# First modulation vectors of a hybrid DeltaNet / gMLP step: weights as the stationary operand

## The chip, the cores and the metric

The kernel runs on one core of a Trainium2 chip. A core has TensorE (matrix products, with a weight load and a matmul instruction for each product), VectorE (DVE), ScalarE (ACT), GpSimd (POOL) and SyncE (SP), which here issues the DMA transfers. The metric is the device time of one execution in microseconds. A profile is one execution taken by the hardware profiler; the time before is the median of three runs.

## The reference

One layer of a backbone over 128 context tokens and 2048 latent tokens, with a model width of 1024. Both kinds of token go through a norm that is scaled and shifted by modulation vectors, a mixer, a gated addition, a second modulated norm and an MLP. What the change touches is the modulation:

```python
def modulation(cond, w_mod_l, b_mod_l):
    m = jax.nn.silu(cond) @ w_mod_l + b_mod_l
    return jnp.split(m[:, None, :], N_MOD, axis=-1)
...
    sh1, sc1, ga1, sh2, sc2, ga2 = mod
    h = rmsnorm(x, norm_mix_l) * (1.0 + sc1) + sh1
```

There are two conditioning vectors, `c_ctx` for the context and `c` for the latent tokens. `w_mod` is 1024 × 6144 in float32. Its first 1024 columns give the shift `sh1`, the next 1024 the scale `sc1`. The kernel needs both as columns: feature number on the partitions, because the normed tokens stand feature-major when they are scaled.

## The kernel before

The kernel is written in Tile. Instructions are written in program order, and a scheduler orders them on each engine before the program is built, by a simulated timeline; each engine then runs its own list in order, and so does SP with its transfers. Tiles come from pools: a tile with `tag` and `bufs` takes one of so many buffers, and a new tile of that tag waits until the oldest is free.

The whole is staged. The first stage (lines 267 to 802, to about 445 us) computes the conditioning vectors, the modulation, the normed and modulated tokens and the projections to q, k, v. Later stages do the gMLP, the DeltaNet scans, the output projection and the MLP. The change lies in the first 40 us.

The steps there, in the order of the code:

- `scond` (line 296) holds silu of the two conditioning vectors, 128 partitions × 8 k-steps × 2 vectors.
- `mod_load` (line 313) issues eight transfers of 128×512 float32 raw weights (256 KB each). It is called for `m0` (shift, first 512 features), `m1` (scale, first 512), and then `m2` and `m3` (shift and scale, second 512), each with its own eight buffers of the pool `wp`.
- `mod_columns` (line 317) turns one such set into columns. Line 321 does eight products: the stationary operand is `scond[:, k, :]` (128×2), the moving operand the raw weights (128×512), and the result, 2×512, gathers in a PSUM bank `pm`. ACT copies it to SBUF as `mrow` (line 323). Four transposes (line 326) write its four 2×128 pieces as 128×2 into a second PSUM bank of the same tag, `pc` in the code and `pm` in the profile. DVE adds the bias from `vec` (line 329) and, for a scale, forms (1 + sc1) · norm weight (line 333), into `b1` or `a1`.
- `xh` (line 363) are ten boundary tokens, loaded by five small transfers and normed; eight transposes (line 373) and a copy make `hal`. `xh` takes one of the three buffers of the tag `x` in the pool `p1`. The same three buffers then serve the three token tiles of the first block (line 377); the third of these waits for the transposes of `xh`.
- `norm_rows` (line 298) norms a token tile: ACT squares and sums, DVE and POOL form the inverse root, DVE scales.
- `first_half(0)` needs the columns of `m0` and `m1`; `column(k)` (line 455) transposes the normed tokens (line 468), scales and shifts them on ACT (line 470) and splits them on DVE into a high and a low part (lines 473, 474). `project(k)` multiplies them with split weights by `mm3` (lines 217 to 219). The first three projections run k = 0 to 3, then come `m2` and `m3`, then k = 4 to 7 in the code's order (lines 728 to 738).
- `pm1()` (line 169) gives one of two PSUM banks of the tag `pm`.

A product in plain float32 is built as two weight loads and two matmul instructions; one in float32r as one of each.

Of the kernel before, what the change touches and what calls it, by code (L numbers as in the profile page):

```python
# [8 lines left out]
F32 = mybir.dt.float32  # L9
# [8 lines left out]
P = 128  # L18
D = 1024
KT = D // P  # L20
# [41 lines left out]
def hybrid_step(  # L62
# [7 lines left out]
    V, A, G, T = nc.vector, nc.scalar, nc.gpsimd, nc.tensor  # L70
# [41 lines left out]
    ident = cp.tile([P, P], F32, name="ident")  # L112
# [49 lines left out]
    scond = cp.tile([P, KT, 2], F32, name="scond")  # L162
# [6 lines left out]
    def pm1():  # L169
        return pmp.tile([P, 512], F32, tag="pm", name="pm", bufs=2)  # L170
# [96 lines left out]
    with ExitStack() as ph:  # L267
        p1 = ph.enter_context(tc.tile_pool(name="p1", bufs=2, reuse_waits="tile"))
        pf = ph.enter_context(tc.tile_pool(name="p1f", bufs=2, reuse_waits="tile"))
# [46 lines left out]

        def mod_columns(raws, half, dst, bias, scaled):

            pm = pm1()
            for k in range(KT):  # L320
                T.matmul(pm[0:2, :], scond[:, k, :], raws[k], start=k == 0, stop=k == KT - 1)  # L321
            row = p1.tile([2, 512], F32, tag="mrow", name="mrow", bufs=1)
            A.copy(row, pm[0:2, :])
            pc = pm1()
            for i in range(4):
                T.transpose(pc[:, 2 * i : 2 * i + 2], row[:, i * P : (i + 1) * P], ident[0:2, 0:2])
            ks = slice(half * 4, half * 4 + 4)
            d = dst[:, :, ks]
            V.tensor_tensor(out=d, in0=pc[:, 0:8].rearrange("p (k c) -> p c k", c=2),
                            in1=bias[:, ks].unsqueeze(1).to_broadcast([P, 2, 4]), op=ALU.add)  # L330
            if scaled:
                for cd in range(2):
                    V.scalar_tensor_tensor(out=dst[:, cd, ks], in0=dst[:, cd, ks], scalar=1.0,
                                           in1=vec[:, 16 + half * 4 : 20 + half * 4], op0=ALU.add, op1=ALU.mult)
# [23 lines left out]
        convw = vec[:, 32:68].rearrange("p (w a) -> p w a", w=3)  # L358
        m1 = mod_load(0, D)
        mod_columns(m0, 0, b1, vec[:, 0:8], False)  # L360


        xh = p1.tile([P, D], F32, tag="x", name="xh", bufs=3)[0:10, :]
        for m in range(5):
            r0 = 255 + 384 * m
            load(out=xh[2 * m : 2 * m + 2, :], in_=x_sample[0, r0 : r0 + 2, :])
# [9 lines left out]
        for t in BLOCKS[0]:  # L376
            x = p1.tile([P, D], F32, tag="x", name="x", bufs=3)
# [341 lines left out]
        m3 = mod_load(1, D)  # L719
        wr = load_w1(1, range(4))  # L720
        mod_columns(m1, 0, a1, vec[:, 8:16], True)
        W1[1] += [split_w(r) for r in wr]
        first_half(0)
# [5 lines left out]
        for k in range(4):  # L729
            cols[k]()  # L730
            for u in us:
                u["main"][k]()
        mod_columns(m2, 1, b1, vec[:, 0:8], False)
        mod_columns(m3, 1, a1, vec[:, 8:16], True)
        W1[1] += [split_w(r) for r in wk]
# [1016 lines left out]
    raws, sops = {}, {}  # L1752
# [91 lines left out]
    for m, (n, i, u, q) in enumerate(todo):  # L1844
# [20 lines left out]
        if i in (1, 5, 6) and mm < 28:  # L1865
            while pending and mm >= pending[0][0] + 2:
                _, k, r = pending.pop(0)
# [60 lines left out]
```

## Time and profile before

| | |
|---|---|
| runs | 2690.73, 2695.26 (median), 2696.66 us |
| profiled execution | 2696.7 us, of which the span from first to last instruction is 2695.0 us |
| mean granted TensorE clock | 0.993 |
| PE busy | 2628.5 us, 98% of the span, 15698 instructions |
| PEld (weight loads) busy | 2192.3 us, 81%, 15698 instructions |
| DVE busy | 1866.8 us, 69% |
| ACT busy | 1245.5 us, 46% |
| POOL busy | 229.5 us, 9% |
| DMA | 580.91 MB, mean 216 GB/s |

How the profile is read: PE is TensorE's matmuls and PEld its weight loads, which overlap them. The ends of matmuls are modelled, and they are pipelined, so a busy PE is not PE at its peak; the distance from one start to the next tells the pace. In a row of the timeline stand the start, the length, the engine, the line, the operation, out<-in, the shape and the count; behind it in brackets how long the engine had been idle and what it waited for. In the shape of a matmul or weight load, `128*2` is the rows and columns of the stationary operand, and behind it stands what was streamed or loaded. In a row of a table of stretches stand the stretch (us), its length, the busy time of each engine with its instruction count (PE, PEld, DVE, ACT, POOL), the granted clock, the busy share of the DMA engines and the GB/s that they moved. The granted clock has no entry ahead of the first change of the clock and shows 1.00 there.

### The profile page before, as it was taken

The numbers are of one execution on the slowest core, as the hardware profiler recorded it, in microseconds if no ns is written. First come the engines' busy times: TensorE is split into PE (matmuls) and PEld (weight loads), VectorE is DVE, ScalarE is ACT, GpSimd is POOL, SyncE is SP. The second block draws the span as 40 slices with busy tenths as digits, with TensorE's granted clock in tenths as the row PEclk, the third lists the DMA queues.
The fourth block names the chain that finished last, engine by engine and source line by source line (L and its number), as shares of the span: only waits on it lengthen the run. The fifth ranks groups of instructions, "written<-read, shape, count | busy, mean of one in ns | idle before, by whom it ended". The sixth has DMA issues, their size and how long they took to land.

```text
span 2695.0 us, 45202 instructions
## 1 busy us (share of the span) xinstructions
PE 2628.5 (98%) x15698; PEld 2192.3 (81%) x15698; DVE 1866.8 (69%) x3909; ACT 1245.5 (46%) x3092; POOL 229.5 (9%) x448
## 2 busy tenths in 40 slices
PE   8999999999999899999999999999999999999998
PEld 5999997788887787778887788888888787888887
DVE  5867656877777878885688775665565547774874
ACT  4655555555555656763355543332342432342441
POOL 3111203111111111110000000000000000000000
PEclk9999999999999999999999999999999999999999
DMA  8867539555555657885877797433459979876772
GB/s 297 279 202 224 183 113 299 177 157 161 160 162 157 204 191 232 269 279 181 285 221 228 212 313 228 122 104 106 121 170 371 329 265 309 272 243 215 235 252 94
DMA packets 569388, 580.91 MB, mean 216 GB/s; under 512 B 35693, under 2 KB 401693, under 8 KB 565575
## 3 DMA queue, kind: packets, MB, share of 16 engines
q1 hardware_dynamic: 569158, 578.03, 67.2%
q8 instruction: 123, 2.02, 0.3%
q14 instruction: 107, 0.87, 0.1%
HBM read 398.14 MB, written 179.74 MB: 214 GB/s over the span
## 4 chain that ended last, share of the span: by engine, by line
PE 86%; DVE 6%; DMA 5%; issue 1%; ACT 1%; POOL 0%; SPq 0%; DVEq 0%; POOLq 0%; ACTq 0%
PE f L219 17%; PE f L217 17%; PE f L218 17%; PE pj L217 6%; PE pj L219 6%; PE pj L218 6%; PE pd L959 3%; PE pm L217 1%; PE pm L219 1%; PE pm L218 1%; PE pm L321 1%; PE pt L575 1%; PE pd L1136 1%; PE pd L1137 1%; DMA qT<-qT_d 1%
## 5 line engine op out<-in xcount | busy, mean ns | idle before, releaser
L217 PE MATMUL f<-hop,zH 128*128 128x512 f32 x960 | 376.5, 393 | 1.2 <-ACT zH L1444 1.2
L218 PE MATMUL f<-hop,zH 128*128 128x512 f32 x960 | 377.1, 393 | 0.0
L219 PE MATMUL f<-hop,zL 128*128 128x512 f32 x960 | 376.9, 393 | 0.0
L217 PE MATMUL f<-hop,wH 128*128 128x512 f32 x896 | 354.0, 397 | 0.0
L219 PE MATMUL f<-hop,wL 128*128 128x512 f32 x896 | 351.3, 392 | 0.0
L218 PE MATMUL f<-hop,wH 128*128 128x512 f32 x896 | 351.1, 392 | 0.0
L1444 ACT CAST zH<-zraw 128x512 fp32r<-128x512 f32 x240 | 146.6, 620 | 287.2 <-DVE zraw L1438 86.4
L217 PEld LDWEIGHTS f<-hop,zH 128*128 128x128 f32 x960 | 180.3, 188 | 43.7 <-ACT zH L1444 1.6
L219 PEld LDWEIGHTS f<-hop,zL 128*128 128x128 f32 x960 | 180.3, 188 | 41.9 <-issue 0.9
L218 PEld LDWEIGHTS f<-hop,zH 128*128 128x128 f32 x960 | 180.2, 188 | 41.8 <-issue 0.9
L1438 DVE TENSOR_TENSOR zL<-zraw,zH 128x512 fp32r<-128x512 f32 x240 | 162.9, 686 | 69.1 <-ACT zH L1444 57.7
L219 PEld LDWEIGHTS f<-hop,wL 128*128 128x128 f32 x896 | 168.5, 188 | 37.7
L218 PEld LDWEIGHTS f<-hop,wH 128*128 128x128 f32 x896 | 168.8, 188 | 35.2
L217 PEld LDWEIGHTS f<-hop,wH 128*128 128x128 f32 x896 | 168.8, 188 | 34.7
L217 PE MATMUL pj<-kH,wH 128*128 128x386 f32 (+2 forms) x568 | 190.5, 338 | 0.3 <-DVE kH L473 0.3
L219 PE MATMUL pj<-kH,wL 128*128 128x386 f32 (+2 forms) x568 | 190.3, 335 | 0.0
L218 PE MATMUL pj<-kL,wH 128*128 128x386 f32 (+2 forms) x568 | 189.5, 334 | 0.0
L176 POOL TENSOR_TENSOR r<-rsq,nhalf 128x1 f32<-128x1 f32 (+1 forms) x38 | 23.0, 606 | 1499.3 <-DVE rsq L175 1499.3
L1438 DVE TENSOR_TENSOR wL<-raw,wH 128x512 fp32r<-128x512 f32 x112 | 76.0, 687 | 76.0 <-ACT wH L1444 74.9
L523 DVE SCALAR_TENSOR_TENSOR cv<-pj,vec,cv 128x384 f32<-128x384 f32 (+2 forms) x164 | 87.1, 539 | 58.7 <-ACT cv L520 57.4
L217 PEld LDWEIGHTS pj<-kH,wH 128*128 128x128 f32 x568 | 107.2, 189 | 4.6 <-issue 4.2
L217 PE MATMUL pj<-wH,hH 128*128 128x512 f32 x248 | 109.8, 443 | 0.0
(398 smaller groups left out, 6088.3 us busy)
## 6 DMA issues: line engine op xcount, KB each, us to landing
zraw<-z_d SPq DMA_DIRECT2D x212, 256.0 KB
raw<-in_w_ff_dram SPq DMA_DIRECT2D x128, 256.0 KB
hop<-hop_d SPq DMA_DIRECT2D x28, 1024.0 KB
z_d<-c SPq DMA_DIRECT2D x96, 256.0 KB
zraw<-s_d SPq DMA_DIRECT2D x96, 256.0 KB
raw<-in_w_mod_dram SPq DMA_DIRECT2D x80, 256.0 KB
r<-in_w_ff_dram SPq DMA_DIRECT2D x80, 256.0 KB
s_d<-s SPq DMA_DIRECT2D x64, 256.0 KB
```

The source lines that it names most:

```text
L176: G.tensor_tensor(out=out, in0=t[:np_, :n], in1=nhalf[:np_, :n], op=ALU.pow)
L217: T.matmul(ps, lh, rh, start=first and i == 0, stop=False, skip_group_check=more)
L218: T.matmul(ps, lh, rl, start=False, stop=False, skip_group_check=more)
L219: T.matmul(ps, ll, rh, start=False, stop=last and i == n - 1, skip_group_check=more)
L321: T.matmul(pm[0:2, :], scond[:, k, :], raws[k], start=k == 0, stop=k == KT - 1)
L523: V.scalar_tensor_tensor(out=cv[:, o : o + m], in0=ps[:, s + sh : s + sh + m], scalar=convw[:, w, j : j + 1], in1=cv[:, o : o + m], op0=AL ...
L575: T.matmul(ps[:, i * P : (i + 1) * P], kTt[:, i * P : (i + 1) * P], rhs[:, i * P : (i + 1) * P], start=True, stop=True)
L959: T.matmul(p[:, h, :], lhs[:, h, :], rhs[:, h, :], start=True, stop=True)
L1136: T.matmul(p[:, h, :], u["qT"][:, h, :], s[:, h, :], start=True, stop=False)
L1137: T.matmul(p[:, h, :], u["QK"][:, h, :], u["vn"][:, h, :], start=s is None, stop=True)
L1438: V.tensor_tensor(out=out, in0=a, in1=b, op=op)
L1444: A.copy(h, src)
```

## The change

In `mod_columns` the operands change places. Each 128×512 raw weight tile is taken in four pieces of 128×128, each piece is the stationary operand, and the moving operand is `scond[:, k, :]`, 128×2. The result of piece i is 128×2, feature-major, in columns 2i and 2i+1 of one PSUM bank, gathered over the eight k-steps. So the copy to `mrow` and the four transposes go, and with them the second PSUM bank of each call. A call had eight products and four transposes; it now has 32 products. The steps on DVE behind it are as before.

The boundary tokens `xh` no longer take a buffer of the tag `x`; they have a buffer of their own in the pool `pf`.

```diff
         def mod_columns(raws, half, dst, bias, scaled):
 
-            pm = pm1()
+            pc = pm1()
             for k in range(KT):
-                T.matmul(pm[0:2, :], scond[:, k, :], raws[k], start=k == 0, stop=k == KT - 1)
-            row = p1.tile([2, 512], F32, tag="mrow", name="mrow", bufs=1)
-            A.copy(row, pm[0:2, :])
-            pc = pm1()
-            for i in range(4):
-                T.transpose(pc[:, 2 * i : 2 * i + 2], row[:, i * P : (i + 1) * P], ident[0:2, 0:2])
+                for i in range(4):
+                    T.matmul(pc[:, 2 * i : 2 * i + 2], raws[k][:, i * P : (i + 1) * P], scond[:, k, :],
+                             start=k == 0 and i == 0, stop=k == KT - 1 and i == 3)
             ks = slice(half * 4, half * 4 + 4)
             d = dst[:, :, ks]
...
-        xh = p1.tile([P, D], F32, tag="x", name="xh", bufs=3)[0:10, :]
+        xh = pf.tile([P, D], F32, tag="xh", name="xh", bufs=1)[0:10, :]
```

## The prediction

> **What bounds the kernel now.** I read the page first, then the chain of waits, then the timeline and the table of stretches for the first 130 us, because the change touches nothing later.
>
> ```profile
> span 2695.0 us, 45202 instructions
> PE 86%; DVE 6%; DMA 5%; issue 1%; ACT 1%; POOL 0%; SPq 0%; DVEq 0%; POOLq 0%; ACTq 0%
> ```
>
> The chain that ended last is TensorE work for 86% of the span. So what the change does to TensorE's time in its stage should reach the end almost in full, if TensorE is the bound in that stage and behind it. The timeline of PE in the stage (start, us):
>
> ```profile
> 4.56 9.38 PE L321 MATMUL pm<-raw,scond 128*2 128x512 f32 x16 [4.56 <-DMA raw<-in_w_mod_dram]
> 15.01 7.03 PE L321 MATMUL pm<-raw,scond 128*2 128x512 f32 x16
> 21.97 0.66 PE L373 MATMUL pt<-ident,xh 10*128 10x10 f32 x8
> 22.56 0.53 PE L468 MATMUL pt<-ident,x 128*128 128x128 f32 x2
> 23.36 7.03 PE L321 MATMUL pm<-raw,scond 128*2 128x512 f32 x16
> 31.11 0.41 PE L326 MATMUL pm<-ident,mrow 2*128 2x2 f32 x4 [0.72 <-ACT mrow L323]
> 31.44 7.03 PE L321 MATMUL pm<-raw,scond 128*2 128x512 f32 x16
> 39.19 0.41 PE L326 MATMUL pm<-ident,mrow 2*128 2x2 f32 x4 [0.46 <-ACT mrow L323]
> 40.57 0.59 PE L217 MATMUL pj<-kH,wH 128*128 128x388 f32 x2 [0.32 <-DVE kH L473]
> ```
>
> The four calls of mod_columns (I name them by their weights m0, m1, m2, m3) fill PE from 4.56 to 39.60, and only then come the projections. A float32 product is two instructions here, hence x16 for eight k. The last three calls run at 0.43 us per instruction, the first takes 9.38 us instead of 7.03. What follows, in stretches (PE, PEld, DVE, ACT and POOL busy, granted clock, DMA share, GB/s):
>
> ```profile
> 38.50:41.00 2.50, 1.72 (x9) 1.11 (x10) 1.48 (x10) 1.89 (x4) 0.00 (x0) 1.00 1.02 343
> 41.00:50.00 9.00, 9.00 (x59) 8.82 (x59) 8.93 (x31) 6.89 (x16) 4.40 (x12) 1.00 0.81 280
> 50.00:60.00 10.00, 10.00 (x60) 9.97 (x59) 9.96 (x29) 6.22 (x14) 4.61 (x9) 1.00 0.56 179
> 80.00:90.00 10.00, 9.43 (x53) 8.19 (x53) 9.09 (x21) 8.91 (x30) 0.85 (x1) 1.00 0.65 190
> 90.00:100.00 10.00, 9.21 (x60) 8.60 (x59) 8.10 (x18) 5.05 (x15) 0.00 (x0) 1.00 0.99 310
> 100.00:110.00 10.00, 9.96 (x63) 9.48 (x62) 5.04 (x13) 8.97 (x30) 4.31 (x23) 1.00 0.91 302
> 110.00:120.00 10.00, 9.72 (x64) 9.21 (x63) 8.19 (x18) 6.15 (x17) 3.93 (x12) 1.00 1.02 341
> 120.00:130.00 10.00, 9.76 (x57) 9.36 (x56) 9.56 (x16) 2.97 (x6) 0.00 (x0) 1.00 0.96 307
> ```
>
> From 41 on PE has no slack to swallow a shift: idle between 80 and 130 is 0.57 + 0.79 + 0.04 + 0.28 + 0.24 = 1.9 us. Shifts of the first stage are carried on.
>
> **Part one: what is removed.** Sixty-four L321 instructions, and behind each call one ACT copy of 0.57 us and four L326 transposes, which PE waits for:
>
> ```profile
> 30.48 0.57 ACT L323 COPY mrow<-pm 2x512 f32<-2x512 f32 x1 [7.82 <-PE pm L321]
> 31.10 0.32 PEld L326 LDWEIGHTS pm<-ident,mrow 2*128 2x128 f32 x4 [1.65 <-ACT mrow L323]
> ```
>
> From the last product of m2 to the first of m3 PE gives 31.44 − 30.39 = 1.05 us to this hop, the same behind m0; behind m1 other transposes fill it, and behind m3 it is 39.60 − 38.47 = 1.1.
>
> **Part two: what is added.** Each call becomes 8 × 4 products of two columns, 64 instructions instead of 16, each with a weight load of 128×128 float32: 256 loads in all. Two moving columns cost next to nothing (0.43 us for 512), so the load sets the pace. The rows nearest to it:
>
> ```profile
> 427.88 0.53 PEld L654 LDWEIGHTS pt<-scr,mcum 128*128 128x128 f32 x4
> 38.40 0.14 PEld L468 LDWEIGHTS pt<-ident,x 128*128 128x128 f32 x1 [0.86 <-DVE wL L192]
> 427.64 0.19 PEld L219 LDWEIGHTS pj<-kH,wL 128*128 128x128 f32 x1
> 929.05 1.81 PEld L959 LDWEIGHTS pd<-vn,kt 128*128 128x128 f32 x8
> 1111.86 0.33 PEld L219 LDWEIGHTS pm<-wH,oL 128*128 128x128 f32 x1
> ```
>
> L654 has the same form (plain float32 weights, 128×128) before a moving operand of only 68 columns: (0.53 − 0.19) / 3 = 0.113 us from load to load. L326's transposes give a lower bound, with 0.14 for one load as in L468's transpose: (0.32 − 0.14) / 3 = 0.06. But a load for a transpose is shorter than the 0.19 of a product in L219, so I take 0.113. At full clock then 256 × 0.113 = 28.9 us, against 64 × 0.43 = 27.5: no gain on the products themselves, only the hops. The last two rows stand in stretches at half clock (in the table below): one load takes 0.33 instead of 0.19, and eight come (1.81 − 0.33) / 7 = 0.211 us apart. Bounds 0.211 and 2 × 0.113 = 0.226; I take 0.216, as those eight also stream 128 columns each: 256 × 0.216 = 55.3 us (54.0 to 57.9).
>
> **Which clock holds** decides the sign. The first call starts at half clock; its loads are 0.86 us apart and become 0.43 apart behind 9.4 us:
>
> ```profile
> 6.22 0.13 PEld L321 LDWEIGHTS pm<-raw,scond 128*2 128x2 f32 x1 [0.73 <-issue]
> 7.08 0.13 PEld L321 LDWEIGHTS pm<-raw,scond 128*2 128x2 f32 x1 [0.73 <-DMA raw<-in_w_mod_dram]
> 9.92 0.09 PEld L321 LDWEIGHTS pm<-raw,scond 128*2 128x2 f32 x1 [0.34 <-issue]
> 10.35 0.09 PEld L321 LDWEIGHTS pm<-raw,scond 128*2 128x2 f32 x1 [0.34 <-issue]
> ```
>
> Later the clock falls to half and rises again in steps of 3.41 us. The table of such stretches, the granted clock third from the right:
>
> ```profile
> 473.55:476.97 3.42, 3.07 (x17) 1.76 (x17) 3.42 (x12) 1.93 (x7) 0.61 (x1) 0.50 0.71 259
> 476.97:480.38 3.41, 2.37 (x19) 1.55 (x18) 3.41 (x12) 3.41 (x9) 1.75 (x3) 1.00 0.25 82
> 920.70:924.11 3.41, 1.84 (x25) 1.21 (x24) 3.41 (x9) 3.41 (x15) 0.40 (x1) 1.00 0.98 331
> 924.11:927.53 3.42, 1.83 (x20) 1.44 (x20) 3.42 (x14) 1.96 (x7) 0.90 (x3) 1.00 0.51 182
> 927.53:930.94 3.41, 2.96 (x24) 2.76 (x23) 3.41 (x16) 1.66 (x4) 1.70 (x3) 0.50 0.37 111
> 930.94:934.35 3.41, 3.41 (x31) 3.11 (x30) 3.20 (x11) 1.01 (x3) 0.90 (x1) 0.50 0.28 79
> 1111.85:1115.26 3.41, 3.41 (x9) 2.65 (x8) 3.31 (x11) 0.25 (x1) 1.62 (x2) 0.50 1.04 369
> ```
>
> Each stretch sets the clock of the next. 920.70 and 924.11 have the same matmul time (1.84 and 1.83); the second has more weight loading (1.44 against 1.21), yet behind it the clock falls. 927.53 has loads in 2.76 of 3.41 us and the clock stays at half; 473.55 has loads in only 1.76, but a little more matmul time (3.07 against 2.96), and the clock rises. So loads don't seem to count, streaming does. That rests on four stretches, and the profile's matmul time has modelled ends, so it is a lean and no proof. The new products stream 2 columns, 0.43 × 2 / 512 = 0.0017 us, per load: under 2% of the time. If only streaming counts, the clock never rises until the projections come.
>
> The Trainium skill, "TensorE: Matmul & The Clock Gate", section "Part 1: The HAM clock gate (the "warmup" mystery)", has the same gate: default half rate, lifted by a busy window of about 3.4 us. It does not say whether a weight load is busy time; read so that it is, its sum would be that of the first rival, read as streaming only, that of the forecast.
>
> **The sum at half clock.** m0 starts at 4.56 as now (first weights landed; a k-step takes 8 × 0.216 = 1.7 us, more than its weights take to land). 4.56 + 55.3 + 2 × (0.66 + 0.53) for the L373 and L468 transposes = 62.3, against 39.60: **+22.7**. The gap from 39.60 to the first projection at 40.57 goes, as the first half's columns are built while m2 and m3 run: **−1.0**. About nine further L468 transposes move into the slow stretch, at some 0.1 us more each (half of 0.211): **+1.0**. The clock lifts one to two stretches of 3.41 us into the projections, half of that lost: 1.7 to 3.4, **+2.3**. Of the 1.9 us idle later a half is regained by loads that have landed earlier: **−1.0** (0 to −1.9). Together **+24.0 us**: 2695.0 of span and 1.7 around it, 2696.7, become 2720.7. The median of the runs is 1.4 under the profiled one, so I predict **2719**; by the bounds 2712 to 2724.
>
> **The xh tile** gets a buffer of its own, so the third x load need not wait for xh's. In SP's order it stands at 27.81, two weight loads late:
>
> ```profile
> 16.03 10.02 SPq L182 DMA_DIRECT2D raw<-in_w_mod_dram  x16
> 27.81 0.33 SPq L378 DMA_DIRECT2D x<-in_x_sample_dram  x1
> 31.80 1.28 ACT L191 CAST wH<-raw 128x512 fp32r<-128x512 f32 x2 [0.75 <-DMA raw<-in_w_in_dram]
> ```
>
> Ahead of the sixteen weight loads, it delays m2, m3 and w_in by its 512 KB, at the 343 GB/s above 1.5 us; PE is still in m1 then, so I cost it at nothing (at full clock w_in lands before m3 ends at 36.9, below: nothing too). The DVE and ACT steps behind the products stay (L329, L333).
>
> **Rivals.** *Weight loads count as busy, full clock from about 9.4 us* (not slower). m0: 22 loads at half rate until 9.34, 42 × 0.113 more: 14.1. m1 21.3, transposes 22.5, m2 29.7, m3 36.9 instead of 39.60; with the 1.0 gap gone −3.7: 2693.0, by the median 2691.6. For it: PE would be occupied without a pause, and matmul shares as low as 1.84 of 3.41 kept the clock. Against: the two pairs above.
>
> *The load is as short as a transposed one, 0.062, at full clock.* Then arrivals bound the stage: w_in's first split begins at 31.80, and with it the projections at about 33.2 instead of 40.57: −7.4, 2689 (median 2688). For it: L326 has 128 columns too. Against: L654.
>
> *The clock rises in between* because column transposes and projections of the first half are ordered between m1 and m3, which streams enough: half way between the two cases, about 2705. Against it: w_in lands only at 31.8.
>
> **Chances.** Half clock 0.58, in between 0.06, full clock 0.28, short loads 0.08. Differences under 0.2% (5.4 us) I call the same. Full clock at −3.7 is mostly within that, a third of it beyond: same 0.19; faster 0.08 + 0.09 = 0.17; slower 0.58 + 0.06 = 0.64. The range takes in the full-clock case and the upper bound of the forecast: 2690 to 2724; the forecast's own is 2712 to 2724.
>
> **What would show it.** Loads of L321's successor 0.21 apart until past 60 us, the granted clock 0.50 or lifted only there, first L217 at about 62: right. Loads 0.11 apart behind 9.4 us: the first rival. 0.06: the second. A first L217 at 62 with an end less than 20 us late would refute the step that nothing behind takes up a shift.

## The result, and the profile after

The changed kernel takes 2720.9 us (median of five runs, 2718.5 to 2725.7), the kernel before, beside it, 2693.8 us (2690.7 to 2696.7). The ratio is 1.0104, with a 95% interval of 1.0092 to 1.0115: about 1% slower. The profiled execution took 2720.5 us, 2718.8 of it span, 23.8 us more than before.

The head of the profile after:

```profile
span 2718.8 us, 45547 instructions
...
PE 82%; DMA 7%; DVE 7%; issue 2%; ACT 1%; SPq 1%; POOL 0%; DVEq 0%; POOLq 0%; ACTq 0%
```

TensorE still holds most of the chain that ended last. In the head that chain now runs through transfers (start, us):

```profile
25.42 5.31 DMA raw<-in_w_mod_dram
30.75 5.39 DMA raw<-in_w_in_dram
...
38.71 2.77 POOL kH L460
41.53 1.01 PE pj L217 x2
```

So the first projection is not released by the new products but by its own weights and by kH, into which POOL copies a boundary column (line 460), about as early as before (40.57). What the new products lose there shows behind it, where they and the projections share TensorE. The timeline of the weight loads of the exchanged products, now line 322 (start, us):

```profile
4.01 18.00 PEld L322 LDWEIGHTS pm<-scond,raw 128*128 128x128 f32 x84 [4.01 <-DVE abW L311]
22.98 9.46 PEld L322 LDWEIGHTS pm<-scond,raw 128*128 128x128 f32 x44
32.85 6.95 PEld L322 LDWEIGHTS pm<-scond,raw 128*128 128x128 f32 x32
45.67 3.42 PEld L322 LDWEIGHTS pm<-scond,raw 128*128 128x128 f32 x26
...
58.25 8.14 PEld L322 LDWEIGHTS pm<-scond,raw 128*128 128x128 f32 x60
```

The first 84 loads come (18.00 − 0.33) / 83 = 0.213 us apart (one load at half clock takes 0.33 us); so do the next 76. The 26 loads behind 45.67 come about 0.13 apart on average. The first two calls last until 32.4, in the kernel before until 22.0. The stretches between show why the pace changes (columns as before; the clock has no entry ahead of its first change, here at 46.56, and shows 1.00 there):

```profile
43.15:46.56 3.41, 3.41 (x15) 3.31 (x15) 2.15 (x6) 2.13 (x5) 2.51 (x12) 1.00 1.00 323
46.56:49.97 3.41, 3.41 (x30) 3.41 (x31) 3.20 (x9) 2.00 (x5) 1.78 (x3) 1.00 1.05 383
49.97:53.39 3.42, 3.42 (x15) 3.42 (x15) 2.16 (x6) 1.64 (x5) 3.42 (x8) 0.50 0.81 270
53.39:56.80 3.41, 3.41 (x12) 3.41 (x11) 2.78 (x9) 3.19 (x7) 0.64 (x3) 0.50 0.60 197
60.22:63.63 3.41, 3.41 (x33) 3.41 (x32) 0.00 (x0) 0.00 (x0) 0.00 (x0) 1.00 0.00 0
63.63:67.04 3.41, 3.41 (x18) 3.41 (x19) 0.45 (x4) 0.00 (x0) 0.00 (x0) 0.50 0.00 0
```

From 43.15 to 46.56 projections of 388 columns and four transposes run, and the clock is up in the next stretch. That stretch is mostly two-column products, and behind it the clock is down. Projections from 51.85 on lift it a second time, at 56.80, and the last sixty loads let it fall again, at 63.63, although PE and PEld show 3.41 of 3.41 us busy. A busy engine in the profile is thus not a busy engine for the clock.

The projections begin here, still at half clock (388 columns, 0.52 us each instead of 0.34):

```profile
41.53 1.01 PE L217 MATMUL pj<-kH,wH 128*128 128x388 f32 x2 [1.64 <-POOL kH L460]
43.74 0.52 PE L218 MATMUL pj<-kL,wH 128*128 128x388 f32 x1
...
45.03 1.05 PE L465 MATMUL pt<-ident,x 128*128 128x128 f32 x4
45.88 3.29 PE L322 MATMUL pm<-scond,raw 128*128 128x2 f32 x26
```

The stage's last projection, first in the changed kernel, then before:

```profile
456.89 0.28 PE L219 MATMUL pj<-kH,wL 128*128 128x258 f32 x1
```

```profile
433.70 0.28 PE L219 MATMUL pj<-kH,wL 128*128 128x258 f32 x1
```

It is 23.2 us later. The end is 23.8 later. Some 21 us are lost in the first 70 us, about 2 around 145 us, and the loss is carried through the rest.

### The profile page after: what moved, and what is told of

It is laid out like the page before. It is cut to its first block, busy times and chain, and to the rows that moved or that the text cites. A ratio compares the mean times of both kernels' runs of the same rounds, so it can differ in the third digit from the quotient of the medians.

```text
span 2718.8 us, 45547 instructions
## 1 busy us (share of the span) xinstructions
PE 2653.5 (98%) x15874; PEld 2241.9 (82%) x15874; DVE 1865.4 (69%) x3909; ACT 1245.9 (46%) x3088; POOL 229.9 (8%) x448
## 4 chain that ended last, share of the span: by engine, by line
PE 82%; DMA 7%; DVE 7%; issue 2%; ACT 1%; SPq 1%; POOL 0%; DVEq 0%; POOLq 0%; ACTq 0%
PE f L219 16%; PE f L217 16%; PE f L218 16%; PE pj L217 6%; PE pj L219 6%; PE pj L218 6%; PE pd L956 2%; DMA qT<-qT_d 1%; PE pm L217 1%; PE pm L219 1%; PE pm L218 1%; DMA raw<-in_w_mod_dram 1%; PE pt L572 1%; PE pd L1133 1%; PE pd L1134 1%
## 5 line engine op out<-in xcount | busy, mean ns | idle before, releaser
L217 PE MATMUL f<-hop,zH 128*128 128x512 f32 x960 | 376.5, 393 | 1.2 <-ACT zH L1441 1.2
L217 PE MATMUL f<-hop,wH 128*128 128x512 f32 x896 | 354.8, 397 | 0.0
L217 PEld LDWEIGHTS f<-hop,zH 128*128 128x128 f32 x960 | 180.4, 188 | 43.7 <-ACT zH L1441 1.6
L217 PEld LDWEIGHTS f<-hop,wH 128*128 128x128 f32 x896 | 169.1, 189 | 34.9
L217 PE MATMUL pj<-kH,wH 128*128 128x386 f32 (+2 forms) x568 | 192.9, 341 | 3.5 <-POOL kH L460 1.6
L217 PEld LDWEIGHTS pj<-kH,wH 128*128 128x128 f32 x568 | 108.1, 191 | 8.7 <-issue 4.9
L217 PE MATMUL pj<-wH,hH 128*128 128x512 f32 x248 | 110.3, 445 | 0.0
```

The costliest lines, as they stand in the source:

```text
L217: T.matmul(ps, lh, rh, start=first and i == 0, stop=False, skip_group_check=more)
```

## The experiments

The theory: a product of two columns streams so little that TensorE's clock neither rises nor stays up, and the weight loads then take twice as long. The rivals: the loads or the number of products cost the time by themselves; the new place of `xh` or the new order does; or only the rise of the clock fails. Eleven kernels were run. All ratios are to the kernel before, run beside them on the same chip. "Stage end" is the start of the last 258-column projection in the profile, 433.7 us before and 456.9 in the changed kernel; it comes from one execution, while the runs of one kernel spread over up to 13 us.

| run | edit | median us | ratio, 95% interval | stage end |
|---|---|---|---|---|
| e1 | xh alone | 2694.6 | 0.9999 (0.9989 to 1.0008) | 434.1 |
| e2 | exchanged operands alone | 2716.8 | 1.0089 (1.0074 to 1.0104) | 451.4 |
| e5 | 32 columns | 2720.3 | 1.0106 (1.0080 to 1.0132) | 452.2 |
| e4 | 64 columns | 2707.8 | 1.0052 (1.0037 to 1.0067) | 444.4 |
| e6 | 88 columns | 2712.7 | 1.0077 (1.0057 to 1.0098) | 446.1 |
| e3 | 112 columns | 2694.9 | 1.0008 (0.9999 to 1.0017) | 434.0 |
| e7 | two calls old, two new | 2715.4 | 1.0085 (1.0054 to 1.0115) | 446.7 |
| e8 | 112 columns, one set on DVE | 2718.7 | 1.0094 (1.0072 to 1.0117) | 458.3 |
| e9 | before, other bank | 2696.3 | 1.0016 (1.0006 to 1.0025) | 440.2 |
| e10 | 112 columns, early products | 2700.2 | 1.0026 (1.0014 to 1.0037) | 434.4 |
| e11 | before, other bank, early products | 2696.0 | 1.0016 (1.0007 to 1.0024) | 438.4 |

**e1: xh alone.** The kernel before with

```diff
-        xh = p1.tile([P, D], F32, tag="x", name="xh", bufs=3)[0:10, :]
+        xh = pf.tile([P, D], F32, tag="xh", name="xh", bufs=1)[0:10, :]
```

> The kernel before with one edit alone: xh in its own buffer, products as before. Theory (the loss is the half clock that the two-column products cannot lift): no loss, 2690 to 2697 us, clock lifted at about 9 us as before. Rival (the earlier third x load reorders the stage and delays weights on the one DMA queue): 5 us or more slower than before, 2699 or above.

Ratio 0.9999: this edit by itself costs nothing.

**e2: the exchange alone.** The changed kernel with `xh` back in the tag `x`.

> The changed kernel with xh back in the shared buffers: operands exchanged alone. Theory (half clock): 2716 to 2724 us, loads 0.21 us apart wherever the clock shows 0.50 or has not risen yet. Rival (much of the loss comes with the xh tile): 2710 or below.

1.0089 against 1.0104: most of the loss, or all, as the intervals of the two overlap. The exchange is what costs. Whether `xh` adds something once the operands are exchanged stays open.

**e3: 112 columns instead of 2.** The stationary operand, the loads and their number stay. The two columns are repeated 56 times in the moving operand, and 110 of each 112 results are never read:

```diff
-                    T.matmul(pc[:, 2 * i : 2 * i + 2], raws[k][:, i * P : (i + 1) * P], scond[:, k, :],
+                    T.matmul(pc[:, 112 * i : 112 * i + 112].rearrange("p (a c) -> p a c", c=2),
+                             raws[k][:, i * P : (i + 1) * P],
+                             scond[:, k, :].unsqueeze(1).to_broadcast([P, 56, 2]),
                              start=k == 0 and i == 0, stop=k == KT - 1 and i == 3)
...
-            V.tensor_tensor(out=d, in0=pc[:, 0:8].rearrange("p (k c) -> p c k", c=2),
+            V.tensor_tensor(out=d, in0=pc[:, 0:448].rearrange("p (k w) -> p w k", w=112)[:, 0:2, :],
```

> The changed kernel, but the moving operand repeats the two columns 56 times, so that every weight load is followed by 112 streamed columns; 110 of them are never read. Loads and instructions are the same in number. Theory (only streaming lifts the clock): 112 columns at half clock stream for 0.19 of some 0.216 us, 87% of the time, above the 0.75 or so that lifted the clock in the kernel before; the clock rises about 9 to 11 us, loads come 0.11 us apart, and the time falls by 24 to 30 us to 2690 to 2697, although TensorE streams 56 times as many columns. Rival (the loads, or the number of instructions, or the new order cost the time by themselves): 2716 or above.

2694.9 us, against 2720.9 for two columns: streaming 56 times as much takes the whole loss away. Its loads, and the stretches around the rise:

```profile
4.11 16.05 PEld L322 LDWEIGHTS pm<-scond,raw 128*128 128x128 f32 x126 [4.11 <-DVE abW L311]
...
27.33 10.80 PEld L322 LDWEIGHTS pm<-scond,raw 128*128 128x128 f32 x96
```

```profile
4.72:8.13 3.41, 3.41 (x18) 3.41 (x18) 0.00 (x0) 0.00 (x0) 3.41 (x30) 1.00 0.98 304
8.13:11.55 3.42, 3.42 (x32) 3.42 (x32) 0.17 (x1) 0.00 (x0) 0.21 (x2) 1.00 1.05 384
```

18 products in one stretch, 32 in the next: the clock rose at 8.13, behind one stretch. The later 96 loads come (10.80 − 0.19) / 95 = 0.112 us apart. The loads don't cost the time by themselves; the clock at which they run does. The new order is not ruled out by this run alone, because the order changed with the width: here all 256 products run ahead of the first projection (38.08), in the changed kernel 36 instructions of the projections run ahead of the last product. With 64 columns, below, it is also 36, and the stage still ends 12.5 us earlier than with two. The 10.7 us that are left there are no more than the half clock accounts for: 160 loads run at it ahead of the first projection, 160 × 0.10 = 16 us.

**e4, e5, e6: 64, 32 and 88 columns.** The same edit with another width.

> As the run with 112 columns, with 64. Theory (a stretch of 3.41 us must stream about three quarters to lift the clock, and 0.38 to keep it): 64 columns stream 0.107 of 0.216 us, half of the time, too little to lift it and enough to keep it. So the first calls run at half clock until projections lift it, and what follows keeps full clock: between, 2702 to 2716. Rival (any streaming lifts it): as with 112 columns. Rival (loads cost the time by themselves): 2716 or above.

> The moving operand repeated to 32 columns. Theory: at full clock 32 columns stream 0.027 of 0.113 us, 24% of the time, under the 0.38 or so that kept the clock in the kernel before; so the clock falls back between the projections as with two columns, 2714 to 2723 us. Rival (64 columns were faster in proportion to what is streamed, without thresholds): half way between 2 and 64 columns, about 2714, and the clock holds after its first rise.

> The moving operand repeated to 88 columns. Theory: at half clock 88 columns stream 0.147 of 0.216 us, 68%, under the three quarters needed; so the clock does not rise in the first two calls, and the time is that of 64 columns, 2703 to 2712. If the bound lies lower than 0.68, the clock rises about 8 to 10 us and the time is that of 112 columns, 2690 to 2697.

These three narrow down what lifts the clock and what keeps it. With 64 columns the first two calls ran at half clock (84 loads in 17.99 us, as with two), projections lifted the clock at 42.05, and it stayed up for 433 us. Two stretches of it that hold nearly nothing but these products, the same with 32 columns below:

```profile
52.29:55.70 3.41, 3.41 (x33) 3.41 (x32) 2.18 (x6) 3.35 (x7) 0.00 (x0) 1.00 0.62 201
55.70:59.12 3.42, 3.42 (x33) 3.42 (x33) 2.40 (x8) 0.38 (x1) 0.00 (x0) 1.00 0.10 34
```

```profile
55.89:59.30 3.41, 3.41 (x33) 3.41 (x32) 0.23 (x1) 0.00 (x0) 0.00 (x0) 1.00 0.00 0
59.30:62.72 3.42, 3.42 (x18) 3.42 (x18) 0.19 (x2) 0.00 (x0) 0.00 (x0) 0.50 0.00 0
```

PE and PEld show the same busy time and the same counts, and only with 32 columns does the clock fall. So loads don't count, and at full clock the bound for keeping lies between 32 and 64 columns, 24% and 48% of the time streamed (at 0.43 us for 512 columns, 0.027 and 0.054 us of the 0.113 from load to load). The rival by which any streaming helps in proportion falls with it: 32 columns are as slow as two (1.0106).

88 columns, 69% at half clock (88 × 2 × 0.43 / 512 = 0.148 of 0.213 us), did not lift the clock from 4.28 to 31.10. It rose at 34.51, behind the first stretch that also held three 128-column transposes:

```profile
27.69:31.10 3.41, 3.41 (x18) 3.41 (x18) 0.00 (x0) 0.00 (x0) 0.00 (x0) 1.00 1.06 392
31.10:34.51 3.41, 3.41 (x19) 3.41 (x18) 0.17 (x1) 0.39 (x1) 0.00 (x0) 1.00 1.05 382
34.51:37.92 3.41, 3.41 (x32) 3.41 (x31) 3.14 (x12) 3.30 (x7) 0.00 (x0) 1.00 0.69 190
37.92:41.34 3.42, 1.25 (x9) 1.06 (x9) 2.29 (x8) 0.01 (x1) 3.11 (x11) 1.00 1.01 323
```

```profile
32.87 0.85 PE L467 MATMUL pt<-ident,x 128*128 128x128 f32 x3
33.51 4.63 PE L322 MATMUL pm<-scond,raw 128*128 128x88 f32 x36
```

So at half clock the bound for lifting lies between 69% and the 88% of 112 columns (0.188 of 0.213). The three transposes fill 0.64 us of the stretch ahead of the rise (32.87 to 33.51); the products stream 69% of the other 2.77, 1.9 us or 56% of the stretch, which is less than in the stretches that lifted nothing, and with the transposes it is 75%. In the changed kernel, likewise, projections fill only 1.9 us (55%) of the stretch ahead of the rise at 46.56, and four transposes another 0.85. The Trainium skill, "TensorE: Matmul & The Clock Gate", section "Part 4: PE-mode transpose", says that transposes don't count as busy in the same way as other products; these two stretches speak for their counting. The time, 2712.7, is just above what was expected (2703 to 2712); its stage end is 1.7 us later than with 64 columns. PE is busy in only 1.25 us of the stretch from 37.92, and the clock is at half again from 41.34 to 44.75.

**e7: two calls old, two new.** `m0` and `m1` as in the kernel before, `m2` and `m3` as in the changed one:

```diff
-        mod_columns(m0, 0, b1, vec[:, 0:8], False)
+        mod_columns_old(m0, 0, b1, vec[:, 0:8], False)
...
-        mod_columns(m1, 0, a1, vec[:, 8:16], True)
+        mod_columns_old(m1, 0, a1, vec[:, 8:16], True)
```

> The first two calls as in the kernel before (512 columns streamed, copy and transposes), the last two as in the changed kernel. Theory (two-column products neither lift nor keep the clock): it rises at about 9 us, falls again one or two stretches of 3.41 us after the last streaming, and the last two calls run mostly at half clock: 6 to 11 us slower than before, 2699 to 2705. Rival (only the lifting fails; loads keep a clock that is up): 2690 to 2697, loads 0.11 us apart in the last two calls.

The stretches around the fall, and the loads:

```profile
23.10:26.51 3.41, 2.67 (x23) 2.46 (x24) 2.17 (x11) 1.02 (x3) 0.54 (x1) 1.00 1.05 393
26.51:29.92 3.41, 3.41 (x19) 3.41 (x18) 1.68 (x7) 0.91 (x2) 2.98 (x21) 0.50 1.05 394
```

```profile
24.51 2.12 PEld L322 LDWEIGHTS pm<-scond,raw 128*128 128x128 f32 x18
26.57 13.81 PEld L322 LDWEIGHTS pm<-scond,raw 128*128 128x128 f32 x64
```

The clock was up at 9.44 and fell at 26.51, two microseconds into the two-column products: the next 64 loads take 13.81 us. The rival that only lifting fails is out. The size was missed: 2715 instead of 2699 to 2705. Of the 20.5 us in the profiled span, 13.0 are there at the stage end, as projections in the following stretches run at half clock too; 7.5 come later, where the order of steps differs. Whether that order costs them was not tried; the four runs spread from 2709.7 to 2721.3.

**e8: one set on DVE.** With 112 columns; `m2` is multiplied and summed over k by VectorE, and TensorE sums over partitions:

```diff
+            if dve:
+                acc = [w512("macc"), w512("macc")]
+                for k in range(KT):
+                    for c in range(2):
+                        if k == 0:
+                            V.tensor_scalar_mul(acc[c], raws[k], scond[:, k, c : c + 1])
+                        else:
+                            V.scalar_tensor_tensor(out=acc[c], in0=raws[k], scalar=scond[:, k, c : c + 1], in1=acc[c],
+                                                   op0=ALU.mult, op1=ALU.add)
+                for c in range(2):
+                    for i in range(4):
+                        T.matmul(pc[:, 112 * i : 112 * i + 2], acc[c][:, i * P : (i + 1) * P], pick[:, c, :],
+                                 start=c == 0 and i == 0, stop=c == 1 and i == 3)
```

> The kernel with 112 columns, but the third set of weights is multiplied and summed over k on DVE (two accumulators of 128x512), and TensorE only sums over the partitions with eight products: 48 loads fewer. Theory (the head is bound by TensorE, with DVE free for 10 us or more there): first projection about 4 us earlier than with 112 columns, 2687 to 2692. Rival (DVE, full from 41 us on, is late with the splits of the projections): 2695 or above.

The time is the rival's, the cause only in part. The waits of TensorE between 30 and 75 us (in total, times, longest), and the longest of them in the timeline:

```profile
PE pj L217 <- ACT wH L191: 8.0, 1, 8.0
PE pm L331 <- DVE macc L327: 5.7, 1, 5.7
PE pj L219 <- DVE wL L192: 4.6, 4, 3.6
```

```profile
33.64 2.62 ACT L191 CAST wH<-raw 128x512 fp32r<-128x512 f32 x4 [6.35 <-DMA raw<-in_w_in_dram]
34.36 0.67 PE L217 MATMUL pj<-kH,wH 128*128 128x388 f32 x1 [8.02 <-ACT wH L191]
```

The first projection is indeed 3.7 us earlier than with 112 columns alone (34.36 instead of 38.08), but it has waited 8.0 us for weights that were still landing, before any accumulation. The other 10.3 us are waits for DVE, where the accumulation runs from 41.3 to 61 us between the splits that the projections need. The clock is at half from 26.46 to 40.11 and from 50.35 to 70.83.

**e9, e10, e11: a search for a version that beats both.** e9 is the kernel before with the transposes in a bank of the other pool:

```diff
-            pc = pm1()
+            pc = pt()
             for i in range(4):
```

> The kernel before with one edit: the transposes of each call write a PSUM bank of the other pool (pt), so that the next call's products need not wait until the copy has freed their own bank. Theory (the hop of about 1.05 us between calls is a wait for the bank): two to three hops go, 2 to 3 us faster than before, ratio 0.9988 to 0.9994. Rival (PE's order puts the transposes ahead of the next products whatever the bank): no change, 0.9995 to 1.0005.

e10 is e3, and e11 is e9, with this ahead of `m0 = mod_load(0, 0)`:

```diff
+        wps = pj().rearrange("p (a b) -> p a b", b=P)
+        for _ in range(6):
+            T.matmul(wps, ident16, bc4(ident16), start=True, stop=True)
+
         m0 = mod_load(0, 0)
```

> The kernel with 112 columns, and six products of 512 f16 columns that nobody reads ahead of the first weights, while TensorE has nothing to do (2.3 to 4.8 us). Theory: the clock rises one stretch of 3.41 us earlier in about three of four executions, up to 1.7 us; 0 to 2 us faster than with 112 columns alone, ratio to before 0.9992 to 1.0008. Rival (the added products push the first weights' products back): 1.0008 or above.

> The kernel before with the bank of the other pool and the six early products. Theory: both gains add, 2 to 5 us faster than before, ratio 0.9982 to 0.9994. Rival (neither shows): 0.9995 to 1.0005.

All three are slower than the kernel before, by 0.16% to 0.26%; neither theory nor rival foresaw that for e9 and e11. In e9 the hop went as meant: the products of the four calls follow one another more closely, and the last begins at 34.67 instead of 37.88. But the gain is given back behind it, where PE waits for the convolution's evacuation on DVE, and DVE for weights still landing:

```profile
132.05 0.41 PE L217 MATMUL pj<-kH,wH 128*128 128x386 f32 x1 [2.87 <-DVE cv L523]
```

The clock is also at half for a stretch from 38.00 and for one from 133.57, behind stretches in which PE was busy in less than half of the time (1.48 of 3.42 and 1.52 of 3.41 us). The stage then ends 6.5 us later than before. In e10 and e11 the early products did lift the clock, at 6.15 and 6.08, but they pushed the first product back (4.95 in e10 instead of 4.14 in e3, as its rival said), TensorE then waited for m2's weights (idle 1.8 and 1.5 us near 22), the clock fell for one stretch at 23.2, and no gain was left at the stage end (434.4 in e10, 434.0 in e3). What e10 loses behind it was not looked into. No version found beats the kernel before; e3 equals it.

## Why the prediction was right

**The outcome.** 2719 was forecast and 2720.9 measured; slower, by the clock.

**What is added: right.** 0.216 us for a load at half clock was taken, 0.213 measured (0.211 was the lower bound). 0.113 at full clock was taken from L654, and e3 has 0.112. That the load sets the pace, and not the two columns, is shown by e3 with e7: 112 columns cost no more per load than two, whose loads come (2.12 − 0.19) / 17 = 0.114 us apart while the clock is up (the row at 24.51 in e7).

**Which clock holds: right, and it was the part least certain.** The two pairs of stretches were called a lean; e4 against e5 shows it with equal loads, e3 shows the rise, e7 the fall. The rival "weight loads count as busy" would have had to show the rise at about 9.4 us; it came at 46.56, behind projections.

**The sum: right in total, wrong in its order.** The step "m0 … m3 at half clock, then the projections at about 62" failed: the first projection stands at 41.53, ahead of most of m2 and m3, as in the third rival, which had been given a chance of 0.06. Of the signs that were named, loads 0.21 apart until past 60 and the first L217 at about 62 did not come. The streaming of the projections lifts the clock in 46.56 to 49.97 and 56.80 to 63.63, so the products together take 47.8 instead of 55.3 us of TensorE's time (the timeline's PE rows of L322 added up). But the projections around them run at half clock in their turn: stretches 41.53 to 46.56, 49.97 to 56.80 and 67.04 to 70.45 hold mostly projections and transposes. I had counted 2.3 us for projections and 1.0 for transposes. The rival took the order rightly and its price (half the loss) wrongly: TensorE spends about 56 us of the head at half clock (4.04 to 46.56, 49.97 to 56.80, 63.63 to 70.45), not far from the 60 of the forecast (4.56 to about 65), only with other work in them.

That the total fits to 0.2 us in the profiled span (+24.0 forecast, +23.8 measured) is luck. The terms of the head add up to +25.0, and the head costs about 21; behind it 1.0 was to be regained, and about 2 more are lost.

**The gap of 1.0 us ahead of the first projection: wrong.** It did not go. PE waits 1.64 us there for the boundary column that POOL copies from `halH` into kH:

```profile
38.71 3.36 POOL L460 CAST kH<-halH 128x1 fp32r<-128x1 f32 x6 [12.90 <-DVE halH L393]
```

**Nothing behind takes up a shift: right.** 23.2 us at the stage end, 23.8 at the end of the span. The regained 1.0 us isn't seen; around 145 us the changed kernel instead waits more (PE idle 0.8 + 1.55 us between 140 and 150), for accumulations on DVE that wait for weights.

**The xh tile at nothing: right**, by itself. e1, 0.9999.

## What to carry to other kernels

Exchanging the operands of a product that is too thin left TensorE's time at full clock about the same here (64 × 0.113 against 16 × 0.43 us a call) but turned streaming into loading, and at the start of the kernel that left TensorE at half clock. Look at what a stretch of 3.4 us streams, not at how busy PE and PEld are. Where thin products cannot be avoided, repeating the moving columns beneath the load may lift the clock at no cost in time: the loads stayed 0.112 us apart, and 112 instead of 2 columns took 26 us off.

## What the runs showed of the hardware that was not expected

As shares of the time, lifting and keeping look like two bounds: 64 columns do not lift the clock in the first 38 us (50% streamed at half clock), yet keep it up through the two stretches on end shown above (48% at full clock). Counted in columns, one bound is enough. A stretch of 3.41 us holds 16 loads at half clock (0.213 apart) and 30 at full clock (0.113 apart). At half clock 64 and 88 columns are then 1020 and 1410 a stretch, and the clock did not rise; 112 are 1790, and it rose. At full clock 32 are 970, and it fell; 64 are 1930, and it held. Any one bound between 1410 and 1790 columns fits all five, and the theory's three quarters at half clock and 0.38 at full clock are about 1520 and 1540 (0.75 × 3.41 / 0.86 × 512 and 0.38 × 3.41 / 0.43 × 512). No run was made to tell one bound from two.

Changes confined to the first 70 us move what comes long behind: from the stage end to the end of the span the kernel before takes 2261.3 us, e9 2251.3, e10 2271.1 in the profiled executions. All execute the same steps there, in an order that the scheduler made anew each time. How much of these 20 us is the order is not shown: each is a single execution, and the eight runs of e10 alone spread over 11 us, the profiled one being the slowest. Either way, an edit of 3 us in the head cannot be judged by one total alone.
